# A fixed order on three engines for the first feed-forward product, with each weight block loaded fewer times

## The chip, the cores and the metric

The kernel runs on one core of a Trainium2 chip. The metric is the time of one execution on the device in microseconds, as the median of several runs. PE is TensorE, DVE is VectorE, ACT is ScalarE, POOL is GpSimd and SP is SyncE; PEld is the row of TensorE's weight loads.

## The reference

The reference is one layer of a streaming encoder with 512 tokens and a width of 2048. An S5 branch and a differential attention branch are gated and added to `x`; after them comes a SwiGLU feed-forward with a hidden width of 5632, which is where the change lies. All is float32.

```python
h = rms_norm(x, norm2_w[l], RMS_EPS)
x = x + (jax.nn.silu(h @ w_ffn_gate[l]) * (h @ w_ffn_up[l])) @ w_ffn_down[l]
```

## The kernel before

Each float32 product is computed in three passes: both operands are split into a high part (`hi`, which ACT rounds with a copy) and a rest (`lo`, which DVE gets by subtracting `hi`), and TensorE computes hi*hi, hi*lo and lo*hi. The method `split` does this for a weight chunk of two 128-row blocks by 512 columns: one instruction on ACT (`whi`) and one on DVE (`wlo`).

The first product of the feed-forward, `h @ [gate, up]`, is done in 11 units (`NU = DFF // T`, unit `u` covers 512 hidden columns of `gate` and of `up`). Within a unit the product is a 2 by 2 block scheme with seven block products instead of eight (Winograd's form of Strassen's scheme). The weights' blocks are `w11` and `w21` (the two halves of the rows of `gate`) and `w12` and `w22` (those of `up`). The products 1 to 7 use `w11`, `w21`, `w22`, and sums of blocks: 7 uses `w12 + w22`, 5 uses `w11 + w12`, 6 adds `w22` to that, 4 adds `w21` to that. The slab `A` holds the running sum. Each block product has four chunks of 12 matmuls: two token halves by two 128-row blocks by three passes. Products 6, 3 and 4 accumulate on the PSUM banks of 1, 5 and 7.

The method `seven` (L1044) issues the chunks of a unit in the order it is given, `(1, (2, 7), 5, (6, 3), 4)` for units 1 to 10; products in one bracket alternate chunk by chunk. For each chunk it calls `weights`, which issues the loads (on SP's queue) and the sums (on DVE), and then the split. Product 4's `w21` is added to `A` in flight by a DMA on POOL's queue (L1317). After a product's last chunk `done` copies or adds its banks to the partial results in the tiles `st` and `act` (L1330 to L1353). After every chunk that is not of product 1, one entry of a list `fill` is issued: four flips of the unit before (`flip_act`: four transposes into a bank and a copy by ACT), five empty entries, and the seven steps of `make`. A step of `make` forms one of the seven operands of the second product out of the flipped unit, splits it into two tiles of the pool `wk` (five tiles, two of which hold the gate for part of the unit) and stores both in DRAM (`opd`, L1271, on POOL's queue), from where the second product (`down`) reads it.

TensorE's instructions stand in the order written. Those of the other engines and queues are ordered by a planner at compile time, which goes by priorities and a model of the times; `behind` ties some steps of `make` behind the latest split. Split weights lie in three pairs of tiles, so a chunk's split waits until the chunk three before it has left TensorE. Loaded blocks lie in a ring of five tiles (`raw`: three of the pool `wp`, two parts of `E`). Unit 0 has its own order, `(1, 7, 2, 5, (6, 3), 4)`, and the operands' preparation beside it; the second product follows unit 10 with the same `seven`.

Of the kernel before, what the change touches and what calls it, by code (L numbers as in the profile page):

```python
# [8 lines left out]
F32 = mybir.dt.float32  # L9
F32R = mybir.dt.float32r  # L10
# [7 lines left out]
P = 128  # L18
# [23 lines left out]
class Block:  # L42
# [998 lines left out]

    OWN = {1: ("lin", "lin"), 7: ("lin", "lin"), 2: ("S", "S"), 5: ("S", "S")}

    def seven(self, n, weights, ops, done, order=ORDER, fill=(), own=OWN):  # L1044

        nc = self.nc
        banks = {}  # L1050
        fill = list(fill)
        for group in order:
            group = group if isinstance(group, tuple) else (group,)
            for i in group:
                banks[i] = [self.bank(t) for t in own[i]] if i in own else banks[{6: 1, 3: 5, 4: 7}[i]]
            for c in range(0, n, 2):
                for i in group:
                    raw = weights(i, c)

                    self.nc3 = (self.nc3 + 1) % 3 if self.fp else 1  # L1060
                    hi, lo = (self.wp.tile([P, 2, T], F32R, tag=t, name=self.uid(t)) if self.nc3 else
                              self.fp.tile([P, 2, T], F32R, tag=t, name=self.uid(t)) for t in ("whi", "wlo"))
                    self.last = self.split(hi, lo, raw)
                    for tt, kk in ((tt, kk) for tt in range(2) for kk in range(2)):
                        k = c + kk
                        xh, xl = (ops[i][:, h, k, tt * P:(tt + 1) * P] for h in range(2))
                        for q, (l, r) in enumerate(((xh, hi), (xh, lo), (xl, hi))):
                            nc.tensor.matmul(banks[i][tt], l, r[:, kk, :], skip_group_check=True,  # L1068
                                             start=(i in own and k == 0 and q == 0), stop=(k == n - 1 and q == 2))
# [148 lines left out]
    def flips(self, parts):  # L1218
# [4 lines left out]
            self.nc.tensor.transpose(tp[:, h * P:(h + 1) * P], z, self.ident)  # L1223
        return tp

    def ffn(self, ops, steps, x2d, out):
        nc, a, tc = self.nc, self.a, self.tc
        NU = DFF // T
# [23 lines left out]
        def flip_act(u, j):  # L1252

            tp = self.flips([act[u, tt][:, j * P:(j + 1) * P] for tt in range(4)])
            nc.scalar.activation(self.E[:, 4 + j], tp, AF.Copy)

        flips_act = lambda u: [lambda j=j: flip_act(u, j) for j in range(4)]

        def make(u):

            x1, x2 = self.E[:, 4:6], self.E[:, 6:8]
            a, b = slice(0, 256), slice(256, 512)

            def step(i, x, op=None):
                def f():
                    if op:
                        self.behind(op())
                    hl = [self.work((P, 2, 256), F32R) for _ in range(2)]
                    self.behind(self.split(*hl, x))
                    for h in range(2):  # L1270
                        pool.dma_start(opd[u, i - 1, :, h], hl[h].bitcast(F32))  # L1271
                return f
# [10 lines left out]
        for u in range(NU):  # L1283
            w = {(k + 1, m + 1): (gate, up)[m][k * 1024:(k + 1) * 1024, u * T:(u + 1) * T] for k in range(2) for m in range(2)}
            st = {}
            first = u == 0

            def weights(i, c):
                for _ in range(2 if i == 2 else 1):
                    if steps:  # L1290
                        steps.pop(0)()
                b = lambda k, m: w[k, m][c * P:(c + 2) * P, :]
                if i == (5 if first else 1) and c == 0:
                    if self.A is None:
                        self.A = self.slab("s5", (P, 8, T), F32)
                A = None if self.A is None else self.A[:, c:c + 2]
                if i == 1:
                    return load(raw() if first else A, b(1, 1))
                if i == 2:
                    return load(raw(), b(2, 1))  # L1300
                if i == 3:
                    return st["w22"]
                if i == 7:
                    r1, r2 = load(raw(), b(1, 2)), load(raw(), b(2, 2))
                    add(dve, r2, r1, r2)
                    if not first:
                        add(dve, A, A, r1)
                    return r2
                if i == 5:
                    if first:  # L1310
                        load(A, b(1, 1))
                        add(dve, A, A, load(raw(), b(1, 2)))
                elif i == 6:
                    st["w22"] = load(raw(), b(2, 2))
                    add(dve, A, A, st["w22"])
                else:
                    pool.dma_start(A, two(b(2, 1)), accum_op=ALU.add)  # L1317
                return A

            def done(i, banks):  # L1320
                if first and i == 6:
                    self.E, self.ring = self.slab("s1", (P, 8, T), F32), 2
                if i == 2 and first or i == 6 and u == NU - 1:
                    self.ring = 0
                for tt in range(2):
                    r = lambda th: self.r2[:, 2 * th + tt:2 * th + tt + 1]
                    p = banks[tt]
                    if i == 1:
                        st["x", tt] = self.work()
                        nc.scalar.activation(st["x", tt], p, AF.Copy)  # L1330
                    elif i == 2:
                        g = st["g", tt] = st["x", tt]
                        add(dve, g, g, p)
                        nc.scalar.activation(g, g, AF.Silu, scale=r(0))
                    elif i == 7:
                        st["q"] = banks
                    elif i == 5:
                        d = st["d", tt] = self.fw() if tt else self.spare("row")
                        nc.scalar.activation(d, p, AF.Copy)
                        add(dve, d, d, st["q"][tt], ALU.subtract)  # L1340
                    elif i == 6:
                        x = st["x", tt] = self.spare(("c16", "s16")[tt])
                        nc.scalar.activation(x, p, AF.Copy)
                        add(dve, st["d", tt], st["d", tt], x, ALU.subtract)
                    elif i == 3:
                        o = act[u, tt] = self.fw()
                        add(dve, o, p, st["x", tt], ALU.subtract)
                        dve.scalar_tensor_tensor(o, o, r(0), st["g", tt], op0=ALU.mult, op1=ALU.mult)
                    elif i == 4:
                        x, d = st["x", tt], st["d", tt]  # L1350
                        add(dve, x, x, p)
                        nc.scalar.activation(x, x, AF.Silu, scale=r(1))
                        dve.scalar_tensor_tensor(d, d, r(1), x, op0=ALU.mult, op1=ALU.mult)  # L1353
                        act[u, 2 + tt] = d
# [147 lines left out]
```

## Time and profile before

| | us |
|---|---|
| median of 3 runs | 2575.45 (2575.34 to 2577.14) |
| the profiled execution | 2580.43 |
| its span, first to last instruction | 2578.7 |
| unit 0 of the first product, about | 1250 to 1334 of the span |
| units 1 to 10 | 1334 to 2129 |
| the second product of the feed-forward | 2129 to 2578.7 |

The span is that of one profiled execution. A busy share counts the time in which an engine has an instruction in work; matmuls overlap in the records. A wait is the idle time of an engine before an instruction, put down to what released it. A tile's name stands for its tag: `whi` and `wlo` are split weights, `wk` a work tile, `lin`, `S`, `T` and `O` are PSUM banks, `s` stands for several slabs (among them `A` and `E`), and `raw` for loaded blocks.

### The profile page before, as it was taken

What the parts mean: (1) busy time and instruction counts of PE and PEld (TensorE: products, weight loads), DVE (VectorE), ACT (ScalarE), POOL (GpSimd) and SP (SyncE); (2) the same over time, 40 slices, a digit from 0 to 9 for tenths busy, and PEclk for the clock granted to TensorE, in tenths of its full rate; (3) what the DMA queues carried; (4) which work ended last, traced back from release to release, by engine and by line L of the source; (5) the groups of instructions that cost most, each with busy time, mean ns of one, the idle gap of its engine ahead of it and who ended that gap; (6) DMA issues with size and microseconds to landing.
All of it is one profiled execution on the core that took longest, in us unless ns stands there. A gap on an engine that the chain in (4) does not pass through costs nothing.

```text
span 2578.7 us, 32198 instructions
## 1 busy us (share of the span) xinstructions
PE 2515.2 (98%) x11655; PEld 2050.2 (80%) x11655; DVE 1907.5 (74%) x3024; ACT 1149.1 (45%) x1540; POOL 316.2 (12%) x491
## 2 busy tenths in 40 slices
PE   8999999999999999999999999999999999999999
PEld 7788887877787678888777888878887887788787
DVE  7888854577777775535778787787777778788788
ACT  4123343354455543323545555555554556333332
POOL 1022310000111110000001111111101111000000
PEclk9999999999999999999999999999999999999999
DMA  6545564666753434433767667767667687867775
GB/s 191 158 131 147 142 200 152 222 219 204 253 192 103 130 119 147 159 115 131 240 166 215 199 197 211 209 196 221 190 205 209 197 288 257 254 205 230 245 230 150
DMA packets 258447, 491.84 MB, mean 191 GB/s; under 512 B 43448, under 2 KB 47864, under 8 KB 258288
## 3 DMA queue, kind: packets, MB, share of 16 engines
q1 hardware_dynamic: 196208, 352.50, 42.2%
q0 software_dynamic: 49504, 133.04, 18.7%
q10 hardware_dynamic: 12576, 4.24, 0.8%
q8 instruction: 92, 1.51, 0.2%
q14 instruction: 67, 0.55, 0.1%
HBM read 420.35 MB, written 71.96 MB: 191 GB/s over the span
## 4 chain that ended last, share of the span: by engine, by line
issue 54%; PE 27%; POOL 7%; DVE 5%; DMA 5%; ACT 1%; ACTq 0%; POOLq 0%; DVEq 0%
PE lin L522 21%; POOL opd L1271 3%; DMA raw<-in_w_in_dram 3%; DVE wlo L531 2%; POOL s L1317 2%; PE lin L1068 1%; POOL s L1426 1%; DVE raw L1082 1%; PE S L715 1%; PE O L745 1%; PE S L472 1%; ACT whi L530 1%; PE S L414 1%; PE S L476 0%; DMA s<-in_w_ffn_down_dram 0%
## 5 line engine op out<-in xcount | busy, mean ns | idle before, releaser
L1068 PE MATMUL lin<-whi,s 128*128 128x512 f32 x2400 | 769.9, 391 | 2.0 <-ACT whi L530 2.0
L522 PE MATMUL lin<-s,whi 128*128 128x512 f32 x2432 | 747.1, 397 | 16.5 <-ACT s L536 7.2
L530 ACT ACTIVATE whi<-s 128x1024 fp32r<-128x1024 f32 x351 | 370.1, 1059 | 424.2 <-PE lin L1068 168.4
L522 PEld LDWEIGHTS lin<-s,whi 128*128 128x128 f32 x2432 | 454.9, 190 | 126.8 <-issue 14.9
L531 DVE TENSOR_TENSOR wlo<-s,whi 128x1024 fp32r<-128x1024 f32 x351 | 428.0, 1222 | 137.6 <-ACT whi L530 136.6
L1068 PEld LDWEIGHTS lin<-whi,s 128*128 128x128 f32 x2400 | 450.7, 188 | 95.9 <-ACT whi L530 3.3
L1068 PE MATMUL lin<-wlo,s 128*128 128x512 f32 x1200 | 470.2, 392 | 10.5 <-DVE wlo L531 10.4
L522 PE MATMUL lin<-s,wlo 128*128 128x512 f32 x1216 | 455.4, 393 | 0.0
L500 DVE TENSOR_TENSOR wlo<-raw,whi 128x1024 fp32r<-128x1024 f32 (+1 forms) x153 | 186.0, 1217 | 211.5 <-ACT whi L499 204.6
L499 ACT ACTIVATE whi<-raw 128x1024 fp32r<-128x1024 f32 (+1 forms) x153 | 161.0, 1053 | 356.7 <-PE lin L522 327.5
L1068 PE MATMUL S<-whi,s 128*128 128x512 f32 x976 | 319.4, 393 | 0.2 <-ACT whi L530 0.2
L530 ACT ACTIVATE whi<-raw 128x1024 fp32r<-128x1024 f32 x190 | 200.0, 1058 | 231.0 <-PE lin L1068 75.6
L1068 PEld LDWEIGHTS lin<-wlo,s 128*128 128x128 f32 x1200 | 225.4, 188 | 65.2 <-DVE wlo L531 19.5
L531 DVE TENSOR_TENSOR wlo<-raw,whi 128x1024 fp32r<-128x1024 f32 x190 | 230.2, 1222 | 58.9 <-ACT whi L530 58.4
L522 PEld LDWEIGHTS lin<-s,wlo 128*128 128x128 f32 x1216 | 230.1, 189 | 48.5
L1068 PEld LDWEIGHTS S<-whi,s 128*128 128x128 f32 x976 | 184.0, 189 | 38.1 <-ACT whi L530 0.6
L1068 PE MATMUL S<-wlo,s 128*128 128x512 f32 x488 | 191.7, 393 | 7.9 <-DVE wlo L531 7.8
L1271 POOL DMA_DIRECT2D opd<-wk x154 | 91.2, 618 | 733.7 <-ACT wk L530 634.6
L1068 PE MATMUL T<-whi,s 128*128 128x512 f32 x400 | 139.7, 390 | 0.5 <-ACT whi L530 0.5
L1068 PE MATMUL O<-whi,s 128*128 128x512 f32 x400 | 139.5, 389 | 0.0
L1068 PEld LDWEIGHTS S<-wlo,s 128*128 128x128 f32 x488 | 92.1, 189 | 29.7 <-DVE wlo L531 11.6
L1233 DVE TENSOR_TENSOR s<-s,raw 128x1024 f32<-128x1024 f32 x79 | 96.5, 1222 | 12.5 <-DMA raw<-in_w_ffn_up_dram 11.3
(409 smaller groups left out, 2741.4 us busy)
## 6 DMA issues: line engine op xcount, KB each, us to landing
raw<-in_w_in_dram SPq DMA_DIRECT2D x175, 512.0 KB, 4.3
raw<-in_w_ffn_up_dram SPq DMA_DIRECT2D x83, 512.0 KB, 4.5
opd<-wk POOLq DMA_DIRECT2D x154, 256.0 KB, 4.5
s<-opd SPq DMA_DIRECT2D x77, 512.0 KB, 9.1
s<-in_w_ffn_down_dram SPq DMA_DIRECT2D x65, 512.0 KB, 6.3
s<-in_w_ffn_gate_dram SPq DMA_DIRECT2D x60, 512.0 KB, 5.0
s<-in_w_ffn_up_dram SPq DMA_DIRECT2D x48, 512.0 KB, 4.2
s<-in_w_ffn_gate_dram POOLq DMA_DIRECT2D x44, 512.0 KB, 8.1
```

Source lines behind the costliest of these rows:

```text
L414: nc.tensor.matmul(mb[:, q * 32:(q + 1) * 32], w1[:, ri, q].rearrange("p k c -> p (k c)"), self.cd[:, ri, q].rearrange("p g c -> p (g c)") ...
L472: state = lambda ri, **kw: nc.tensor.matmul(y[:, q * P:(q + 1) * P], w2[:, ri, q].rearrange("p k c -> p (k c)"), sd[:, ri, q].rearrange("p ...
L499: nc.scalar.activation(hi[:, ks], raw[:, ks], AF.Copy)
L500: nc.vector.tensor_tensor(lo[:, ks], raw[:, ks], hi[:, ks].bitcast(F32), op=ALU.subtract)
L522: nc.tensor.matmul(acc[b], l, r, start=(k == 0 and i == 0), stop=(k == nk - 1 and i == 2))
L530: ins = self.nc.scalar.activation(hi, x, AF.Copy)
L531: self.nc.vector.tensor_tensor(lo, x, hi.bitcast(F32), op=ALU.subtract)
L715: nc.tensor.matmul(sp[m], qT[ms, h, i * P:(i + 1) * P], kT[ms, h, 0:W], start=True, stop=True)
L1068: nc.tensor.matmul(banks[i][tt], l, r[:, kk, :], skip_group_check=True, start=(i in own and k == 0 and q == 0), stop=(k == n - 1 and q == 2))
L1233: add = lambda eng, o, x, y, op=ALU.add: eng.tensor_tensor(o, x, y, op=op)
L1271: pool.dma_start(opd[u, i - 1, :, h], hl[h].bitcast(F32))
L1317: pool.dma_start(A, two(b(2, 1)), accum_op=ALU.add)
```

## The change

Units 1 to 10 leave `seven` and the loop with `weights` and `done`, and are issued by a new method `units`, inside a block in which DVE and ACT, too, keep the order written. SP's and POOL's queues are still ordered by the planner.

- The products stand in the order `(1, 2), (7, 5, 3, 6), 4`. Product 3 has banks of its own (T and O), product 5 takes the S banks, and an add (`53`) joins them.
- Time is counted in chunks. In step `s` of the loop TensorE gets chunk `s`, ACT and DVE split chunk `s + 2`, and DVE forms the sums for chunk `s + 4`. Between ACT's and DVE's half of the split stand the steps due (`post`): evacuations of banks one to four steps after a product's last chunk (`STAGES`), and pieces of `make`.
- The blocks `w21`, `w12` and `w22` of a unit come once each into the ring of five, a load being issued when its place is given free; `w11` goes into `A` when product 4 has split the chunk of it. Product 4's `w21` still comes by the adding DMA.
- The flips stand after the chunks 4 to 7 of the next unit, with ACT's copy one step later. The steps of `make` start at step 9 of the unit and stand three steps apart; DVE's half and the stores come one step after ACT's half.
- Unit 0 keeps `seven`, with product 3 on banks of its own, so it also does the add `53`.

```diff
-                    hi, lo = (self.wp.tile(...) if self.nc3 else self.fp.tile(...) for t in ("whi", "wlo"))
+                    hi, lo = self.halves()
...
+    def units(self, ops, block, load, stage, stages, flip_act, make):
...
+        order = ((1, 2), (7, 5, 3, 6), (4,))
+        S = [(u, i, c) for u in range(1, NU) for g in order for c in range(0, 8, 2) for i in g]
+        own = {1: ("lin", "lin"), 7: ("lin", "lin"), 2: ("S", "S"), 5: ("S", "S"), 3: ("T", "O")}
...
+        def sums(u, i, c):
+            a = A[:, c:c + 2]
+            if i == 7:
+                add(a, a, w[u, 1, 2, c])
+                add(w[u, 1, 2, c], w[u, 1, 2, c], w[u, 2, 2, c])
+            elif i == 6:
+                add(a, a, w[u, 2, 2, c])
+
+        def taken(u, i, c):
+            if i == 2:
+                give(u, 2, 1, c)
+            elif i == 7:
+                give(u, 1, 2, c)
+            elif i == 3:
+                give(u, 2, 2, c)
+            elif i == 6:
+                nc.gpsimd.dma_start(A[:, c:c + 2], block(u, 2, 1, c).rearrange("(k p) c -> p k c", p=P), accum_op=ALU.add)
+            elif i == 4 and u + 1 < NU:
+                base(u + 1, c)
...
+            for f, s in zip(make(u - 1, lambda f: at(self.slot + 1, f)), range(s0 + 9, s0 + 40, 3)):
+                at(s, f)
...
+        for s in range(-4, len(S) + 4):
+            self.slot = s
+            if 0 <= s + 2 < len(S):
+                x = src(*S[s + 2])
+                hl[s + 2] = self.halves()
+                nc.scalar.activation(hl[s + 2][0], x, AF.Copy)
+            for f in post.pop(s, ()):
+                f()
+            if 0 <= s + 2 < len(S):
+                hi, lo = hl[s + 2]
+                self.last = nc.vector.tensor_tensor(lo, x, hi.bitcast(F32), op=ALU.subtract)
+                taken(*S[s + 2])
...
+            if 0 <= s + 4 < len(S):
+                sums(*S[s + 4])
+            loads()
+            if 0 <= s < len(S):
...
+                self.chunk(banks[i], ops[i], *hl.pop(s), c, 8, i in own)
...
+        STAGES = {1: ((1, "1"),), 2: ((1, "2"), (2, "gate1")), 7: (), 5: ((1, "5"), (2, "57")), 3: ((2, "53"),),
+                  6: ((1, "6"), (2, "o"), (3, "d"), (4, "act1")), 4: ((1, "4"), (2, "gate2"), (3, "act2"))}
...
-            order = (1, 7, 2, 5, (6, 3), 4) if first else (1, (2, 7), 5, (6, 3), 4)
-            self.seven(8, weights, ops, done, order, flips_act(u - 1) + [lambda: None] * 5 + make(u - 1) if u else (),
-                       own={**self.OWN, 5: ("T", "O")})
+        self.seven(8, weights, ops, done, (1, 7, 2, 5, (6, 3), 4), own={**self.OWN, 5: ("T", "O"), 3: ("S", "S")})
+        with tc.manual_schedule(engines={mybir.EngineType.PE, mybir.EngineType.DVE, mybir.EngineType.Activation}):
+            self.units(ops, block, load, stage, STAGES, flip_act, make)
```

More of the change, by code (lines that the diff above doesn't have):

```diff
@@ L1042, with halves, chunk @@
     OWN = {1: ("lin", "lin"), 7: ("lin", "lin"), 2: ("S", "S"), 5: ("S", "S")}
+    def halves(self):
+        self.nc3 = (self.nc3 + 1) % 3 if self.fp else 1
+        return [(self.wp if self.nc3 else self.fp).tile([P, 2, T], F32R, tag=t, name=self.uid(t)) for t in ("whi", "wlo")]
+    def chunk(self, banks, op, hi, lo, c, n, own):
+        for tt, kk in ((tt, kk) for tt in range(2) for kk in range(2)):
+            k = c + kk
+            xh, xl = (op[:, h, k, tt * P:(tt + 1) * P] for h in range(2))
+            for q, (l, r) in enumerate(((xh, hi), (xh, lo), (xl, hi))):
+                self.nc.tensor.matmul(banks[tt], l, r[:, kk, :], skip_group_check=True,
+                                      start=(own and k == 0 and q == 0), stop=(k == n - 1 and q == 2))
     def seven(self, n, weights, ops, done, order=ORDER, fill=(), own=OWN):
@@ L1058, in seven @@
                     raw = weights(i, c)
-                    self.nc3 = (self.nc3 + 1) % 3 if self.fp else 1
-                    hi, lo = (self.wp.tile([P, 2, T], F32R, tag=t, name=self.uid(t)) if self.nc3 else
-                              self.fp.tile([P, 2, T], F32R, tag=t, name=self.uid(t)) for t in ("whi", "wlo"))
+                    hi, lo = self.halves()
                     self.last = self.split(hi, lo, raw)
[L1064 to L1069, printed above, removed]
+                    self.chunk(banks[i], ops[i], hi, lo, c, n, i in own)
                     if c == n - 2:
@@ L1250, in load, with flip_act, make @@
             return dst
[L1252 removed]
+        def flip_act(u, j, later=lambda f: f()):
             tp = self.flips([act[u, tt][:, j * P:(j + 1) * P] for tt in range(4)])
[L1255 removed]
+            later(lambda: nc.scalar.activation(self.E[:, 4 + j], tp, AF.Copy))
         flips_act = lambda u: [lambda j=j: flip_act(u, j) for j in range(4)]
[L1259 removed]
+        def make(u, later=None):
             x1, x2 = self.E[:, 4:6], self.E[:, 6:8]
@@ L1264, in step, with store, low, f @@
             def step(i, x, op=None):
[L1265 to L1269, printed above, removed]
+                def store(hl):
                     for h in range(2):
                         pool.dma_start(opd[u, i - 1, :, h], hl[h].bitcast(F32))
+                def low(hl):
+                    add(dve, hl[1], x, hl[0].bitcast(F32), ALU.subtract)
+                    store(hl)
+                def f():
+                    o = op() if op else None
+                    hl = [self.work((P, 2, 256), F32R) for _ in range(2)]
+                    if later:
+                        nc.scalar.activation(hl[0], x, AF.Copy)
+                        later(lambda: low(hl))
+                    else:
+                        if o:
+                            self.behind(o)
+                        self.behind(self.split(*hl, x))
+                        store(hl)
                 return f
@@ L1281, in make @@
                     step(4, x22)]
[L1283 to L1315, printed above, removed]
-                else:
[L1317 to L1354, printed above, removed]
-            order = (1, 7, 2, 5, (6, 3), 4) if first else (1, (2, 7), 5, (6, 3), 4)
-            self.seven(8, weights, ops, done, order, flips_act(u - 1) + [lambda: None] * 5 + make(u - 1) if u else (),
-                       own={**self.OWN, 5: ("T", "O")})
@@ new lines, in ffn, with weights @@
+        block = lambda u, k, m, c: (gate, up)[m - 1][(8 * k - 8 + c) * P:(8 * k - 6 + c) * P, u * T:(u + 1) * T]
+        st = {}
+        def weights(i, c):
+            for _ in range(2 if i == 2 else 1):
+                if steps:
+                    steps.pop(0)()
+            b = lambda k, m: block(0, k, m, c)
+            if i == 5 and c == 0:
+                self.A = self.slab("s5", (P, 8, T), F32)
+            A = None if self.A is None else self.A[:, c:c + 2]
+            if i == 1:
+                return load(raw(), b(1, 1))
+            if i == 2:
+                return load(raw(), b(2, 1))
+            if i == 3:
+                return st["w22"]
+            if i == 7:
+                r1, r2 = load(raw(), b(1, 2)), load(raw(), b(2, 2))
+                add(dve, r2, r1, r2)
+                return r2
+            if i == 5:
+                load(A, b(1, 1))
+                add(dve, A, A, load(raw(), b(1, 2)))
+            elif i == 6:
+                st["w22"] = load(raw(), b(2, 2))
+                add(dve, A, A, st["w22"])
+            else:
+                pool.dma_start(A, two(b(2, 1)), accum_op=ALU.add)
+            return A
@@ new lines, in ffn, with done @@
+        STAGES = {1: ((1, "1"),), 2: ((1, "2"), (2, "gate1")), 7: (), 5: ((1, "5"), (2, "57")), 3: ((2, "53"),),
+                  6: ((1, "6"), (2, "o"), (3, "d"), (4, "act1")), 4: ((1, "4"), (2, "gate2"), (3, "act2"))}
+        def done(i, banks):
+            if i == 6:
+                self.E, self.ring = self.slab("s1", (P, 8, T), F32), 2
+            if i == 2:
+                self.ring = 0
+            for tt in range(2):
+                st[f"p{i}", tt] = banks[tt]
+            if i != 3:
+                for _, name in STAGES[i]:
+                    if name not in ("o", "act1"):
+                        stage(0, st, name)
+            else:
+                for name in ("53", "o", "act1"):
+                    stage(0, st, name)
```

76 lines of the change are left out of this document (added).

## The prediction

> **What bounds the kernel now.** I read the engines' totals first, then the stretch that the change rewrites (units 1 to 10 of the first feed-forward product) by windows, then single matmuls, then the waits, and last one stall from the transfer that starts it to TensorE. First the page's totals, then busy time in windows of that stretch (length, then busy us and instructions of PE, PEld, DVE, ACT, POOL, the granted clock, DMA share, GB/s). Each window runs from the first matmul of a unit's product 2 to that of the next unit's; the last ends with the stretch; "sum" adds eleven windows, the first of them the four chunks of unit 1's product 1.
>
> ```profile
> PE 2515.2 (98%) x11655; PEld 2050.2 (80%) x11655; DVE 1907.5 (74%) x3024; ACT 1149.1 (45%) x1540; POOL 316.2 (12%) x491
> ...
> 1345.00:1426.07 81.07, 79.12 (x353) 64.42 (x352) 63.21 (x66) 41.09 (x49) 12.74 (x18) 1.00 0.70 207
> 1426.07:1505.05 78.98, 78.53 (x353) 64.50 (x352) 62.22 (x65) 41.09 (x49) 12.65 (x18) 1.00 0.71 208
> ...
> 1662.98:1743.43 80.45, 78.88 (x353) 64.41 (x352) 62.40 (x65) 41.07 (x49) 12.66 (x18) 1.00 0.69 203
> ...
> 2061.46:2129.30 67.84, 67.56 (x305) 55.56 (x304) 52.88 (x56) 34.91 (x42) 12.75 (x18) 1.00 0.88 280
> sum 795.18, PE 786.93 PEld 644.87 DVE 621.38 ACT 411.06 POOL 126.93; mean PE 71.54 PEld 58.62 DVE 56.49 ACT 37.37 POOL 11.54
> ```
>
> TensorE bounds the kernel, and its clock is full (1.00). The question is how much of these 795.2 us is lost. Matmul records overlap, so I take it from their pace: two starts 24 matmuls apart where nothing waits, and two starts around a chunk that has a flip (four transposes) behind it.
>
> ```profile
> 1305.04 0.39 PE L1068 MATMUL lin<-whi,s 128*128 128x512 f32 x1
> ...
> 1310.48 0.39 PE L1068 MATMUL lin<-whi,s 128*128 128x512 f32 x1
> ...
> 1348.08 0.48 PE L1068 MATMUL lin<-whi,s 128*128 128x512 f32 x1
> ...
> 1351.30 0.48 PE L1068 MATMUL S<-whi,s 128*128 128x512 f32 x1
> ```
>
> The first pair of rows is two chunks apart, so a chunk of 12 matmuls takes 5.44/2 = 2.72 us; I call that a slot. The second pair shows 3.22 us with a flip, so a flip costs 0.50. A unit is 7 products of 4 chunks and 4 flips: 28 x 2.72 + 4 x 0.50 = 78.16 us at least. Ten units need 781.6 and took 795.2: 13.6 us are lost. The windows show it unit by unit: 2.9 in unit 1, 0.8 in unit 2, 2.3 in the one from 1662.98. By busy time the loss would look like 795.18 - 786.93 = 8.3 us.
>
> The Trainium skill, page "Perfetto Trace Analysis", section "Identifying the Most-Contended Engine", calls matmul busy time a poor measure of headroom since matmuls are pipelined; the two numbers above agree (8.3 by busy time, 13.6 by pace), and by busy time the sum below would end 5.3 us higher.
>
> Now the waits inside 1334 to 2129 us (waiter, what it waited for, total us, times, longest): first what held up TensorE's weight loads, then what held up the two engines that feed it.
>
> ```profile
> PEld lin L1068 <- DVE wlo L531: 8.3, 12, 1.4
> PEld T L1068 <- DVE wlo L531: 7.6, 9, 1.1
> PEld T L1068 <- ACT whi L530: 0.9, 1, 0.9
> ...
> ACT wk L530 <- DMA opd<-wk: 57.6, 21, 4.4
> ...
> DVE wk L531 <- DMA opd<-wk: 21.0, 15, 4.4
> DVE raw L1233 <- DMA raw<-in_w_ffn_up_dram: 19.2, 12, 3.2
> DVE s L1233 <- DMA s<-in_w_ffn_up_dram: 13.7, 15, 1.5
> DVE s L1233 <- DMA raw<-in_w_ffn_up_dram: 8.2, 12, 2.0
> ```
>
> TensorE waits only for split weights, 22 times, never for a bank or a transfer of its own. ACT and DVE wait for stores of `opd` to land (78.6 us) and DVE for weights (41.1 us). One stall, followed through the timelines of ACT, DVE, PE and PEld:
>
> ```profile
> 1709.37 0.63 ACT L530 ACTIVATE wk<-s 128x512 fp32r<-128x512 f32 x1 [2.45 <-DMA opd<-wk]
> ...
> 1710.98 1.23 DVE L531 TENSOR_TENSOR wlo<-raw,whi 128x1024 fp32r<-128x1024 f32 x1 [2.41 <-ACT whi L530]
> ...
> 1712.26 0.19 PEld L1068 LDWEIGHTS T<-wlo,s 128*128 128x128 f32 x1 [1.01 <-DVE wlo L531]
> ...
> 1714.40 0.69 DVE L531 TENSOR_TENSOR wk<-s,wk 128x512 fp32r<-128x512 f32 x1 [1.06 <-DMA opd<-wk]
> ...
> 1714.90 0.39 PE L1068 MATMUL lin<-whi,s 128*128 128x512 f32 x1
> ...
> 1716.28 0.19 PEld L1068 LDWEIGHTS lin<-wlo,s 128*128 128x128 f32 x1 [1.41 <-DVE wlo L531]
> ...
> 1715.10 1.06 ACT L530 ACTIVATE whi<-s 128x1024 fp32r<-128x1024 f32 x1 [2.26 <-PE O L1068]
> ```
>
> ACT stands at a piece of `make` (the split of the unit's output) because the work tile it writes is still being stored to `opd`; the weight split behind it comes late, so does DVE's half, and the array idles about 1 us. `make` issues its seven steps in seven slots in a row, with five work tiles of which two hold the gate.
>
> **The change, part by part.** Durations used (busy us, then mean ns of one; after the bar idle time before them):
>
> ```profile
> L531 DVE TENSOR_TENSOR wlo<-s,whi 128x1024 fp32r<-128x1024 f32 x208 | 253.3, 1222 | 73.5 <-ACT whi L530 73.0
> ...
> L531 DVE TENSOR_TENSOR wk<-s,wk 128x512 fp32r<-128x512 f32 x70 | 48.2, 689 | 22.0 <-DMA opd<-wk 21.0 <-ACT whi L530 1.0
> ...
> L1348 DVE SCALAR_TENSOR_TENSOR fw<-fw,rs,wk 128x512 f32<-128x512 f32 x20 | 15.0, 748 | 0.0
> ...
> L530 ACT ACTIVATE whi<-s 128x1024 fp32r<-128x1024 f32 x208 | 219.4, 1058 | 197.7 <-PE lin L1068 67.9 <-PE O L1068 50.1 <-PE S L1068 34.5
> ...
> L530 ACT ACTIVATE wk<-s 128x512 fp32r<-128x512 f32 x70 | 43.8, 626 | 74.5 <-DMA opd<-wk 57.6 <-DVE s L1233 12.9 <-DVE wlo L531 3.7
> ```
>
> TensorE: 28 chunks and 4 flips a unit as before; nothing gained or lost in its own work. Product 3 gets banks of its own, so 2 adds of 0.69 a unit are new on DVE; they are read off the path below. Loads: 20 transfers of 512 KB a unit in place of 24 (w22 no longer comes twice, w12 still once, and four of the twenty still add in flight through POOL). The DMA share of 0.7 leaves room either way, so the fewer bytes I cost at nothing.
>
> The order on DVE. A slot gives DVE 2.72 us. In slot s ACT splits chunk s+2 once chunk s-1 has left TensorE (three buffer pairs): 0.2 after the slot's start in the row at 1715.10 against the matmul at 1714.90, plus 1.06, so DVE's half can start at about 1.5 at the latest. It must be done when chunk s+2 asks for it, 5.44 + 0.23 later than the slot's start. The heaviest place is slots 7 to 9 of a unit. Slot 7: split to 2.7, one sum (1.22) to 3.9, that is 1.2 into slot 8. Slot 8: two adds of product 2's banks to 2.6, split to 3.8, two sums to 6.2, that is 3.5 into slot 9. Slot 9: split to 4.7, against 5.67. It holds by 1.0 us. Slots 24 to 28 carry about 3.3 each (two adds, a piece of `make`, a split), and no sums, so the split there ends at 4.4 or earlier. In all DVE gets 68 instructions for the 66 of a unit before, some 64 us of 78: no stall from its own work. Banks: product 5 starts in slot 9 on those that the two adds of slot 8 empty, the first at 1.9, due at 2.72; product 4 starts in slot 24 on those read in slot 23.
>
> `make` goes to every third slot, 8.2 us apart, its DVE half one slot later. The first tile of a step is wanted again by the next step's DVE half, so a store has about 8.1 us. The sum transfer for product 4 gets tighter: chunk 6 of A is free when product 6's last split ends (2.7 into slot 21) and product 4 needs it split by slot 27: 6 x 2.72 - 2.7 - 2.2 (both halves) = 11.4 us, one slot less than before. The next unit's first block has 4 x 2.72 - 2.3 = 8.6 us to ACT's split, and that split has a further slack of 2. Times from issue to landing, min/median/max: stores of `opd` (these units), sum transfers on POOL (these units), all loads of SP (whole feed-forward):
>
> ```profile
> DMA to landing us min/median/max: 2.3/4.2/9.6
> ...
> DMA to landing us min/median/max: 5.9/8.4/9.5
> ...
> DMA to landing us min/median/max: 3.5/4.8/13.7
> ```
>
> Medians clear all three, and the sum transfers clear even at their longest. POOL's queue is passed by the same 14 stores and 4 sums a unit, 12.7 us of 78. On SP a load waits for a buffer that DVE's split frees; nothing more urgent stands behind it, since the sums for a chunk are due five slots (13.6 us) later. If the stalls from `make` go, the sum transfer is late next, with 1.9 us to spare.
>
> Unit 0 keeps the planner, but gets the two adds too: 0 to 1.4 us; I take 1.4, since TensorE waits for DVE there (rows below). The entry into the fixed order: between 0 and unit 1's loss before, 2.9; I take 1.0, as the mean unit lost 1.4. The third product's order is planned anew by unchanged code: it could gain or lose; its waits, and unit 0's above them:
>
> ```profile
> PEld T L1068 <- DVE wlo L531: 3.1, 3, 2.0
> PEld lin L1068 <- DVE wlo L531: 2.9, 3, 1.5
> ...
> PEld lin L1068 <- DVE wlo L531: 7.4, 9, 1.7
> PEld S L1068 <- DVE wlo L531: 5.9, 5, 1.3
> PEld lin L1068 <- ACT whi L530: 3.3, 4, 2.4
> ```
>
> I take 0 there, between -2.5 and +2.5, the spread that equal units show among themselves (78.9 to 81.1, rounded up).
>
> The sum: -13.6 + 1.4 + 1.0 = -11.2 us. The profiled execution took 2580.43 us (span 2578.7), 5.0 above the median of 2575.45; it would be 2569.2, and the median 2564.3.
>
> **Rivals.** (a) Half the loss stays. DVE waited 41.1 us for weights beside 78.6 for stores; if the spacing cures stores only, 41.1/119.7 = 34% of 13.6 us, 4.7, remain: 2569. For it: the loads still go through a ring of five. Against: each now has five slots.
> (b) The gain is lost further on. If the third product's waits (16.6 in its three rows) grow by half, 8.3 us return: 2564.3 + 8.3 = 2572.6, within 0.2% of before. For it: the planner's order there depends on what is ready. Against: its code and its input times hardly change.
> (c) Slower: a transfer that comes late at the head of a queue whose order is now fixed. The place is the sum transfer for product 4's last chunk, the point 11.4 us. Were it as slow as SP's slowest load, 13.7, each unit would lose 2.3 us, ten 23: 2587. Against: 40 of them took 5.9 to 9.5.
> The Trainium skill, page "TensorE: Matmul & The Clock Gate", section "Architectural detail: the array is 16× 32×32, not 1× 128×128", states that ScalarE's and VectorE's queues are strictly first in, first out; the rows at 1709 to 1716 agree, and it is why (c) has a chance of its own.
>
> **How the numbers follow.** A measurement here tells about 0.2%, 5.2 us, from no change. The sum's case 0.60, whose own range is 2559 (all 13.6 back and 2.5 in the third product) to 2569; (a) 0.13; (b) 0.16; (c) 0.11. Faster by over 0.2% (below 2570.3) is the sum's case and most of (a), 0.70; same 0.18; slower 0.12. The range 2559 to 2577 leaves out most of (c) and a little below.
>
> **What would show it.** Unit windows of 78.2 to 78.8 us; TensorE's waits for split weights in the units under 4 us in place of 16.8; ACT's and DVE's waits for `opd` near 0; no wait of ACT for the POOL sums. It is wrong if units still take 79 us or more, if the first matmuls of product 5 wait for S banks, if splits in slot 9 come late, or if the time past 2129 us grows.

## The result, and the profile after

| | before | after |
|---|---|---|
| median of 6 runs, us | 2578.94 (2575.34 to 2581.35) | 2564.69 (2560.87 to 2570.00) |
| ratio, 95% interval | 1 | 0.9949 (0.9933 to 0.9964) |
| profiled execution, us (span) | 2580.43 (2578.7) | 2570.00 (2568.2) |
| unit 0, first matmul to unit 1 | 70.7 | 69.9 |
| units 1 to 10 | 795.2 | 780.8 |
| second product, to the end | 449.4 | 453.3 |

The kernel is 0.51% faster (0.36 to 0.67%), 13 us by the ratio; the two profiled executions are 10.5 us of span apart. A repeat beside later runs gave 0.9954 (0.9941 to 0.9967).

First the page's totals after, then windows of the changed kernel (length, then busy us and instructions of PE, PEld, DVE, ACT, POOL, the granted clock, DMA share, GB/s): units 1 to 10, two short stretches at the start of the second product, and the second product as a whole.

```profile
PE 2513.2 (98%) x11655; PEld 2055.4 (80%) x11655; DVE 1927.1 (75%) x3046; ACT 1145.1 (45%) x1540; POOL 316.5 (12%) x491
...
1334.08:2114.87 780.79, 780.79 (x3522) 646.33 (x3521) 640.60 (x670) 407.08 (x490) 127.19 (x180) 1.00 0.66 186
...
2120.50:2124.00 3.50, 1.22 (x6) 0.61 (x5) 3.50 (x5) 0.98 (x2) 0.00 (x0) 0.99 0.02 5
2124.00:2127.50 3.50, 3.50 (x10) 2.74 (x9) 2.28 (x3) 1.65 (x2) 0.00 (x0) 0.52 0.45 150
2114.87:2568.20 453.33, 437.24 (x1929) 356.10 (x1927) 374.04 (x412) 177.42 (x185) 31.60 (x34) 0.99 0.70 223
```

In units 1 to 10 PE is busy for the whole 780.79 us, where it was for 786.93 of 795.18 before, and a unit takes 78.08. The page's totals do not show it: 98% then and now. Of the waits in these units, these are the rows of DVE and ACT that matter; no row of PE or PEld is left, and nothing waits for a store to `opd`.

```profile
DVE wlo L1306 <- ACT whi L1301: 135.0, 147, 2.3
...
ACT whi L1301 <- DMA raw<-in_w_ffn_up_dram: 4.9, 3, 1.7
...
ACT whi L1301 <- DMA s<-in_w_ffn_gate_dram: 0.9, 1, 0.9
```

The 3.9 us given back lie behind unit 10. From the first flip in the second product to the second flip (2120.31 to 2127.86) the changed kernel takes 7.6 us, where the kernel before takes 3.2 (2134.75 to 2137.93). The timelines there, of PE and then of DVE:

```profile
2121.92 0.33 PE L1229 MATMUL O<-ident,fw 128*128 128x128 f32 x1 [1.12 <-DVE fw L1464]
2122.02 0.47 PE L1055 MATMUL lin<-whi,s 128*128 128x512 f32 x1
2123.65 0.57 PE L1055 MATMUL lin<-wlo,s 128*128 128x512 f32 x1 [1.16 <-DVE wlo L531]
2124.01 1.05 PE L1055 MATMUL lin<-whi,s 128*128 128x512 f32 x2
...
2119.98 1.22 DVE L531 TENSOR_TENSOR wlo<-s,whi 128x1024 fp32r<-128x1024 f32 x1
2121.12 0.74 DVE L1464 SCALAR_TENSOR_TENSOR fw<-fw,rs,s 128x512 f32<-128x512 f32 x1
2121.78 0.68 DVE L1334 TENSOR_TENSOR s<-s,S 128x512 f32<-128x512 f32 x1
2122.38 1.22 DVE L531 TENSOR_TENSOR wlo<-raw,whi 128x1024 fp32r<-128x1024 f32 x1
```

The first flip of unit 10 waits for the last gating (`fw`, L1464), the first chunk of product 7 for its split (`wlo<-raw`); on DVE a split of a later product stands ahead of both. DVE has work without a gap from 2109.9 to 2124.7; before, it stood idle for 1.7 us ahead of the split at 2123.9, 5.4 us before the second product began. Then TensorE runs at half its clock: 0.52 granted in the second short window, matmuls 427 ns apart.

### The profile page after: what moved, and what is told of

Same layout as the page of the kernel before. It is cut to its first block, busy times and chain, and to the rows that moved or that the text cites. A ratio compares the mean times of both kernels' runs of the same rounds, so it can differ in the third digit from the quotient of the medians.

```text
span 2568.2 us, 32111 instructions
## 1 busy us (share of the span) xinstructions
PE 2513.2 (98%) x11655; PEld 2055.4 (80%) x11655; DVE 1927.1 (75%) x3046; ACT 1145.1 (45%) x1540; POOL 316.5 (12%) x491
## 4 chain that ended last, share of the span: by engine, by line
PE 43%; issue 39%; POOL 6%; DVE 5%; DMA 5%; ACT 1%; POOLq 0%; ACTq 0%; SPq 0%; DVEq 0%
PE lin L522 30%; PE lin L1055 5%; POOL opd L1369 3%; DMA raw<-in_w_in_dram 3%; PE S L1055 2%; DVE wlo L531 2%; POOL s L1280 1%; POOL s L1556 1%; PE S L715 1%; ACT whi L530 1%; DVE raw L1088 1%; PE S L472 1%; PE O L745 1%; PE S L414 1%; PE S L476 0%
## 5 line engine op out<-in xcount | busy, mean ns | idle before, releaser
L522 PEld LDWEIGHTS lin<-s,whi 128*128 128x128 f32 x2432 | 455.3, 190 | 127.7 <-issue 14.8
L1055 PEld LDWEIGHTS lin<-whi,s 128*128 128x128 f32 x2400 | 452.3, 188 | 96.0 <-ACT whi L530 2.8
L1055 PE MATMUL S<-whi,s 128*128 128x512 f32 x1328 | 436.0, 393 | 0.2 <-ACT whi L530 0.2
L1055 PEld LDWEIGHTS S<-whi,s 128*128 128x128 f32 x1328 | 250.5, 189 | 52.3 <-ACT whi L530 0.6
L1055 PE MATMUL S<-wlo,s 128*128 128x512 f32 x664 | 260.5, 392 | 8.5 <-DVE wlo L531 8.5
L531 DVE TENSOR_TENSOR wlo<-raw,whi 128x1024 fp32r<-128x1024 f32 x118 | 142.1, 1220 | 32.6 <-ACT whi L530 32.1
L1055 PEld LDWEIGHTS S<-wlo,s 128*128 128x128 f32 x664 | 125.4, 189 | 37.0 <-DVE wlo L531 11.8
```

The costliest lines, as they stand in the source:

```text
L522: nc.tensor.matmul(acc[b], l, r, start=(k == 0 and i == 0), stop=(k == nk - 1 and i == 2))
L531: self.nc.vector.tensor_tensor(lo, x, hi.bitcast(F32), op=ALU.subtract)
L1055: self.nc.tensor.matmul(banks[tt], l, r[:, kk, :], skip_group_check=True, start=(own and k == 0 and q == 0), stop=(k == n - 1 and q == 2))
```

## The experiments

Each was run beside the kernel before on its chip. "Nine units" is the time from the first flip in unit 1 to that in unit 10; a window of that length gives it for the two kernels, before and after:

```profile
sum 716.46, PE 708.49 PEld 580.29 DVE 560.38 ACT 369.98 POOL 114.17; mean PE 708.49 PEld 580.29 DVE 560.38 ACT 369.98 POOL 114.17
...
sum 702.68, PE 702.68 PEld 581.69 DVE 577.14 ACT 366.28 POOL 114.50; mean PE 702.68 PEld 581.69 DVE 577.14 ACT 366.28 POOL 114.50
```

The first number is the length. So 13.8 us are to be explained. Theory: the stalls came from `make` standing at stores of `opd`, and its new spacing cured them. Rivals: it is the order on DVE and ACT, or the fewer loads.

**Spaced make alone, in the old loop.**

```diff
-flips_act(u - 1) + [lambda: None] * 5 + make(u - 1) if u else ()
+flips_act(u - 1) + [lambda: None] + [g for f in make(u - 1) for g in (f, lambda: None, lambda: None)][:-2] if u else ()
```

> The kernel before with one edit: the seven steps of make stand at every third entry of the fill list (5, 8, ... 23) in place of seven in a row; loads, product order and the planner's order on DVE and ACT stay. Units 1 to 10 took 795.2 us before and 780.8 after the change. Spacing theory (ACT and DVE wait for stores to opd, 78.6 us): ACT's and DVE's waits for opd fall below 10 us and most of the 14.4 us come back, units 782 to 785, the kernel 10 to 13 us below before. Rival (a), the loads count too: a third of the loss stays, units 786 to 788, 8 to 9 us below. Fixed-order theory (it is the order on DVE and ACT that saves the time): units 791 or more, within 4 us of before.

Ratio to before 0.9996 (0.9983 to 1.001): nothing. Its nine units, one bad unit, its waits, and that unit's stall in the timelines of DVE, SP and PEld:

```profile
1345.78:2062.79 717.01, 707.27 (x3170) 582.08 (x3168) 562.19 (x586) 369.05 (x441) 114.08 (x162) 1.00 0.70 205
1742.52:1825.47 82.95, 80.25 (x354) 65.63 (x352) 62.86 (x66) 41.12 (x49) 12.66 (x18) 0.98 0.70 203
...
DVE raw L1233 <- DMA raw<-in_w_ffn_up_dram: 38.5, 19, 5.7
...
DVE s L1233 <- DMA s<-in_w_ffn_up_dram: 28.5, 18, 4.5
PEld T L1068 <- DVE wlo L531: 13.5, 9, 3.1
...
1788.87 1.22 DVE L1233 TENSOR_TENSOR raw<-raw,raw 128x1024 f32<-128x1024 f32 x1 [5.66 <-DMA raw<-in_w_ffn_up_dram]
1790.01 1.22 DVE L531 TENSOR_TENSOR wlo<-s,whi 128x1024 fp32r<-128x1024 f32 x1
...
1779.91 0.37 SPq L1249 DMA_DIRECT2D raw<-in_w_ffn_up_dram  x1
...
1791.28 0.19 PEld L1068 LDWEIGHTS T<-wlo,s 128*128 128x128 f32 x1 [3.12 <-DVE wlo L531]
```

The waits for `opd` are gone, as the theory said, and the time did not move. In the units 1 to 9 one stall each is left, always at the third chunk of product 3, and it has another origin: the planner put the sum for the next unit's product 7 on DVE ahead of this chunk's split, and that sum's load, issued at 1779.91, landed at 1788.9. DVE waits for weights 76 us (38.5 + 28.5 + 9.3) where it had waited 41. A wait took the place of the one removed, at about the same size. (Behind the longest stall TensorE ran at half clock for 3.4 us, the 0.98 in the second row; that is at most 1.7 us of the 717.)

**Spaced make with the sums tied behind the splits.** As above, and in units 1 to 10 each sum stands behind the split of the chunk before.

```diff
-add(dve, A, A, st["w22"])
+o = add(dve, A, A, st["w22"])
+if not first:
+    self.behind(o)
```

> The run with spaced make alone, with one more edit: in units 1 to 10 each sum of weight blocks is tied behind the split of the chunk before it, so that the planner can't put it earlier on DVE; the planner orders the rest. In the run with spaced make alone no engine waited for opd any more, and the loss sat in one stall a unit (0.85 to 3.1 us, nine times): DVE stood at the sum for the next unit's product 7, whose load was still landing, with product 3's split behind it. Theory Q (two causes, stores at the head of ACT's queue and early sums at the head of DVE's): the stall goes, units 1 to 10 at 782 to 785 us, the kernel 9 to 13 us below before. Rival (only a whole fixed order does it): units stay at 790 or more, within 4 us of before.

Ratio 0.9967 (0.9954 to 0.9979). Nine units, and the waits that are left:

```profile
sum 709.16, PE 704.35 PEld 581.30 DVE 562.57 ACT 367.24 POOL 113.46; mean PE 704.35 PEld 581.30 DVE 562.57 ACT 367.24 POOL 113.46
...
PEld S L1068 <- DVE wlo L531: 7.1, 6, 2.4
...
DVE s L1233 <- DMA s<-in_w_ffn_up_dram: 25.2, 12, 3.4
DVE raw L1233 <- DMA raw<-in_w_ffn_up_dram: 25.1, 18, 3.2
```

The stall at product 3 is gone and 7.3 of the 13.8 us are back. Neither theory's number is met (units at 782 to 785, or 790 and more; the nine at 709 make about 787 for ten). So one cause is shown: sums at the head of DVE's queue, 7.9 us against the run before (717.01 to 709.16). That stores at the head of ACT's queue are the other one in the old loop is read from the waits only; a run with the sums tied and `make` still in a row was not made. All waits left are at splits of product 2; at the longest, 2.4 us, a sum whose load was still landing stood ahead of the split on DVE (3.4 us idle at 1599).

**The changed kernel with DVE and ACT given back to the planner.**

```diff
-with tc.manual_schedule(engines={mybir.EngineType.PE, mybir.EngineType.DVE, mybir.EngineType.Activation}):
+with tc.manual_schedule(engines={mybir.EngineType.PE}):
```

> The changed kernel with one edit: only TensorE keeps the order written, DVE and ACT are ordered by the planner again; product order, single loads and spaced make stay. Spacing theory: units 1 to 10 stay at 781 to 784 us, the kernel within 3 us of the changed one. Fixed-order theory: the stalls come back, units 790 or more, the kernel 8 to 14 us above the changed one. Of the third product's start both say nothing; the planner may order it otherwise, -4 to +2 us.

Ratio to before 1.0086 (1.0073 to 1.01): slower than before by 22 us. Nine units, and what TensorE's weight loads waited for:

```profile
sum 731.92, PE 713.73 PEld 582.41 DVE 572.60 ACT 371.04 POOL 114.40; mean PE 713.73 PEld 582.41 DVE 572.60 ACT 371.04 POOL 114.40
...
PEld S L1055 <- DVE wk L1334: 15.2, 10, 2.4
PEld lin L1055 <- DVE wlo L1306: 9.8, 10, 1.4
PEld lin L1055 <- ACT whi L1301: 4.7, 7, 1.5
```

The new product order needs the S banks emptied within one slot, and the planner does not do that: product 5 waits for them once in every unit. Without the order on DVE and ACT the nine units take 29 us more, and the kernel is over 30 us above the changed one, more than the 8 to 14 expected. ACT and DVE waited for stores of `opd` again, too (53.4 and 7.9 us): the planner did not keep the spacing (the steps of `make` start 2.4 to 7.2 us apart on ACT), so the run takes away both.

**The changed kernel with make in a row.**

```diff
-range(s0 + 9, s0 + 40, 3)
+range(s0 + 13, s0 + 20)
```

> The changed kernel with one edit: the seven steps of make stand in seven steps in a row (13 to 19 of a unit) in place of every third; the fixed order, product order and single loads stay. Spacing theory: a step's tile is still being stored when the next step writes it (store landing 4.2 us against a slot of 2.72), and in a fixed order the splits stand behind it: each of seven steps is late by about 2 us, less some 3 us of slack, 2 to 12 us a unit, the kernel 20 to 120 us above the changed one, with ACT's or DVE's waits for opd the largest. Fixed-order theory: units stay at 781 to 784.

Ratio 1.0461 (1.0448 to 1.0475), 119 us above before. Its rows:

```profile
sum 817.02, PE 742.81 PEld 598.92 DVE 580.27 ACT 366.55 POOL 113.91; mean PE 742.81 PEld 598.92 DVE 580.27 ACT 366.55 POOL 113.91
...
DVE wk L1334 <- DMA opd<-wk: 106.6, 32, 8.2
...
PEld S L1055 <- DVE wlo L1306: 53.2, 18, 5.1
```

12.7 us a unit are lost, a little more than was expected. Part of it is the clock: 0.96 was granted over these units, which is at most some 33 of the 114 us (an estimate, 4% of 817). In the planner's order the same seven steps in a row cost at most the 1.4 us a unit of the kernel before. A fixed order does not remove a late operand; it makes everything behind it pay. The spacing alone brought nothing in the old loop, and the order without the spacing does harm; in the changed kernel both are needed.

**Steps of make two apart.** `range(s0 + 9, s0 + 40, 2)`.

> The changed kernel with the steps of make two steps apart (5.4 us) in place of three (8.2). Spacing theory: a store lands 4.2 us after its issue (2.3 to 9.1), so most steps find their tile free; ACT's and DVE's waits for opd appear but stay under 15 us in all, units 1 to 10 at 781 to 784 us. The last unit ends with less left on DVE, so the second product's start may lose 0 to 2 us less than its 4. A threshold theory (the spacing must exceed a store's longest landing, 9.1): units 785 or more.

Ratio 0.9956 (0.9941 to 0.997). Nine units took 702.68 us, as with three apart, although waits for stores appear:

```profile
ACT wk L1379 <- DMA opd<-wk: 9.0, 9, 3.2
...
DVE wk L1334 <- DMA opd<-wk: 3.0, 4, 1.2
```

5.4 us of spacing against a median landing of 4.2 suffices; 12 us of waits are hidden by the two chunks of lead. The second product did not gain: the first flip waited 3.6 us there instead of 1.4.

**As many loads as before.** Four copies of 512 KB a unit from a block of `w22` to an unread place in DRAM, on SP's queue.

```diff
+if 0 <= s < len(S) and S[s][1] == 6:
+    nc.sync.dma_start(idle[s // 4 % 4], block(S[s][0], 2, 2, S[s][2]).rearrange("(k p) c -> p k c", p=P))
```

> The changed kernel with 4 more transfers of 512 KB a unit on SP's queue (a block of w22 copied to a place in DRAM that nobody reads), so that a unit issues 24 as before. If the fewer loads matter by their number or bytes, units 1 to 10 go from 780.8 to 785 us or more; by the sum of the prediction, which costs them at nothing, they stay at 780.8 to 782 and the kernel within 2 us of the changed one.

Inconclusive: nine units took 702.67 us, the kernel 0.9972 (0.9962 to 0.9983) of before, but the copies did not run in the units. SP's queue is the planner's, and it issued all 40 at the start of the kernel (duration in ns, then first and last start in us):

```profile
L1315 SPq DMA_DIRECT2D idle<-in_w_ffn_up_dram x40: 542/548/2256, 19.2 to 127.0; - x40
```

So whether the fewer loads are needed beside the order and the spacing is left open. Alone they are not enough: in the run with DVE and ACT given back to the planner, which has the fewer loads, DVE waited 84.5 us for weights (36.6 + 26.7 + 14.8 + 6.4), more than the 41 before. The new product order was never taken away by itself.

**Two more instructions on DVE in step 8 of each unit**, repeats of the split's second half, ahead of the sums.

```diff
+if s % 28 == 8:
+    for _ in range(2):
+        nc.vector.tensor_tensor(lo, x, hi.bitcast(F32), op=ALU.subtract)
```

> The changed kernel with two repeats of the DVE half of a split (1.22 us each) in step 8 of each unit, ten units. The prediction's ledger has 1.0 us to spare in slot 9 by durations; back to back DVE starts them 1.14 apart, which leaves about 1.5. By durations each unit is late by 1.3 us (13 in all), by pace by 0.7 (7 in all); if the order has more slack than the ledger says, nothing. If DVE's load were no limit at all, no stall at any place.

```profile
sum 705.96, PE 705.49 PEld 581.41 DVE 596.82 ACT 366.08 POOL 114.51; mean PE 705.49 PEld 581.41 DVE 596.82 ACT 366.08 POOL 114.51
...
PEld lin L1055 <- DVE wlo L1306: 5.0, 10, 0.7
```

Each unit is late once, by 0.36 us (705.96 - 702.68 over nine). 2 x 1.14 us were added, so the slack there was 1.9 us, not 1.0: the ledger found the right place and was 0.9 too strict.

**The adding transfer three steps later.**

```diff
-nc.gpsimd.dma_start(A[:, c:c + 2], ...)
+at(self.slot + 3, lambda: nc.gpsimd.dma_start(A[:, c:c + 2], ...))
```

> The changed kernel with product 4's adding transfer issued three steps later than the place becomes free; for the last chunk of each unit that cuts its time from 11.4 us to 11.4 - 3 x 2.72 = 3.3 us, while such a transfer lands in 6.1 us (5.8 to 8.8). If the ledger's budget is right, ACT waits for it and each unit is late by 2.8 us, or by 1.9 if this ledger too is 0.9 too strict, as it was for DVE (two repeats cost 0.36 us a unit in place of 1.3): 19 to 28 us in all. If the fixed order had slack that the ledger doesn't know, less than 10.

Inconclusive: nine units 702.68 us, ratio 0.9957 (0.9942 to 0.9973), but the edit moved nothing. The transfers' first and last start, after and in this run:

```profile
L1280 POOL DMA_DIRECT2D s<-in_w_ffn_gate_dram x40: 1177/1235/1276, 1364.1 to 2098.7; - x40
...
L1280 POOL DMA_DIRECT2D s<-in_w_ffn_gate_dram x40: 1177/1235/1276, 1361.9 to 2096.5; - x40
```

Counted from the first flip of unit 1 (1347.68 and 1345.46) both start at 16.4 us. POOL's queue is still the planner's, and it issues the transfer when its place is free, wherever the line stands. What a late sum transfer would cost is left open.

**The start of the second product, three tries.** With ACT's splits tied to the order of the chunks there:

```diff
+new = self.split(hi, lo, raw)
+if self.tied and i != order[0]:
+    self.behind(new)
```

> The changed kernel with one edit: in the second feed-forward product ACT's splits are tied to the order of the chunks (the planner had put the split of product 5's first chunk before that of product 7's). Theory P, the planner's reversal makes the wait at 2122 us: the wait for wlo there (1.16) goes, the one of the flip (1.12) gets shorter, and the stretch at half clock behind them (1.8 us lost) goes with them: the second product 450 to 451 us in place of 453.3, the kernel 2 to 3.5 us below the changed one. Rival D, DVE itself is full there (busy without a gap from 2109.9 to 2124.7): within 1 us of the changed one.

Ratio 0.9965 (0.9954 to 0.9977). Start to start, the first flip's gap fell from 1.39 to 0.35 us, that of product 7's split rose from 1.63 to 2.23; from the first flip to the second it took 7.1 us in place of 7.6, and the second product 456.1. The reversal by the planner is not the cause.

With the flips one chunk later and make's steps two apart (`fill = [lambda: None] + flips_act(NU - 1)`):

> The changed kernel with make's steps two apart and unit 10's flips one chunk later in the second product (behind product 7's chunk in place of product 2's). With the steps two apart alone the flip waited 3.6 us at 2114.5 for the last gating on DVE, while the split for product 7 was ready 0.6 us after TensorE asked for it; behind product 7 the flip finds the gating nearly done. If the wait of the flips is what the second product lost (453.3 us in place of 449.4), 3 us come back: 445 to 446 us from the first flip's old place to the end, where the run with steps two apart had 448.4. If DVE's load is the bound there, the wait moves to the split of the next chunk and less than 1 us comes back.

Ratio 0.995 (0.9937 to 0.9962). The second product, and the waits of weight loads in its first 28 us and in the 65 us after them:

```profile
2106.93:2562.60 455.67, 438.01 (x1929) 355.73 (x1927) 373.85 (x412) 177.21 (x185) 31.75 (x34) 0.99 0.70 222
...
PEld lin L1055 <- DVE wlo L531: 1.3, 3, 0.5
...
PEld lin L1055 <- DVE wlo L531: 4.7, 4, 1.7
PEld lin L1055 <- ACT whi L530: 3.8, 3, 2.3
```

The waits at the start fell to 1.3 us (2.9 in the changed kernel), and the product as a whole took 455.7 us in place of 453.3: most of it was lost again at the change to the next pass, some 80 us on, where TensorE fell to half clock (as it did there in the changed kernel, at 2202). The third try adds the tie to it:

> The run with late flips and, in the second product's first pass, ACT's splits tied to the order of the chunks, so that product 7's split stays ahead of product 5's whatever the planner finds. If the planner keeps that order by itself in the run with late flips, the same time within 1 us; if not, 1 to 3 us less.

Ratio 0.9958 (0.9946 to 0.9971), the second product 454.7 us. None of the three beats the changed kernel, which was run beside the last two:

> The changed kernel itself, on the chip of the runs beside it: 0.994 to 0.996 of before. Units 1 to 10 at 780.8 us again, the second product's start with the same waits.

Ratio 0.9954 (0.9941 to 0.9967); units 1 to 10 at 780.79 us again, the second product at 454.9. No version here is faster than the changed kernel by more than the intervals.

Other runs tell more of the loss at the start of the second product. With DVE and ACT given back to the planner the first flip there is 3.2 us ahead of the second, as before, and the second product takes 450.8 us: the loss comes with the fixed order. In the run with the copies, whose second product has the code of the changed kernel, the same two waits stand at 2117.90 and 2119.63, and no half clock follows. Its windows over the waits and behind them:

```profile
2116.70:2120.20 3.50, 1.41 (x8) 0.77 (x6) 3.50 (x5) 0.95 (x2) 0.00 (x0) 1.00 0.02 5
2120.20:2123.70 3.50, 3.50 (x19) 2.89 (x18) 2.28 (x3) 2.78 (x4) 0.00 (x0) 1.00 0.51 150
```

There the two flips are 5.8 us apart. So of the 4.4 us that the changed kernel lost at this place, the waits are 2.6 and the half clock most of the rest, and the half clock comes in some executions and not in others.

## Why the prediction was right or wrong, point by point

- **The loss in the units**, 13.6 us from the pace of the matmuls: right, 14.4 came back. The minimum of 78.16 us a unit was 0.08 too high (a flip costs 0.48, not 0.50). By busy time, 8.3 us, it would have been missed by 6.
- **What makes the loss**: half right. The stores of `opd` stood at the head of ACT's queue, but curing them alone brings nothing, since sums on DVE that wait for loads then cost the same. Rival (a), that a third of the loss would stay if only the stores were cured (its heading says half), used the right mechanism and a wrong size: in the old loop all of it stays. In the changed kernel none does. There the sums stand behind the split and four chunks ahead of their use, which is the likely reason; the fewer loads may have a part in it, and no run tells.
- **The ledger of slots**: right in its verdict and its place; the slack in slot 9 is 1.9 us and not 1.0. (DVE gets 67 instructions a unit for 65 by the counts over ten units, not 68 for 66.)
- **Spacing of make, stores 8.1 us against 4.2**: right; two steps apart would do as well.
- **Fewer loads at nothing**: untested, since the copies that were to show it ran elsewhere.
- **Unit 0, +1.4, and the entry, +1.0**: wrong, both are nothing. Unit 0 took 0.8 us less than before and unit 1 its 78.1 from the first chunk.
- **The second product, 0 with ±2.5**: this term was mis-sized; it lost 3.9, outside its bounds. The bound was taken from the spread of equal units, but the term is not one of them: the fixed order leaves DVE more to do at the end of unit 10 than the planner did, and waits can bring TensorE's clock down behind them. Over the profiled executions with fixed order, spaced `make` and this second product it took 452.3 to 455.0 us, and behind the old loop 447.6 to 449.4. Rival (b) had named the stretch; half of its price came. And a sign of being wrong that the prediction had set, a longer time past the units, did come.
- **The sum**: -11.2 us forecast, -10.5 between the profiled executions and -13 by the runs. By terms it is -14.4 in the units, -0.8 in unit 0, +3.9 in the second product, and +0.8 ahead of unit 0, which the change leaves as it was. It is right in part by luck: the 3.9 lost and the 2.4 that were not lost in unit 0 and the entry, with 0.8 more from the units, largely cancel. That the median of 2564.69 meets the forecast of 2564.3 is luck as well, since the kernel before took 2578.94 in the median of six runs, 3.5 more than the forecast started from.
- **Rival (c)**: not seen (ACT waited for the adding transfers once, 0.9 us); the run that was to bring it about left the transfers where they were. But its mechanism, a late operand in a fixed queue, is what the run with make in a row shows, at 12.7 us a unit, with stores in its place.

## What to carry to other kernels

Before an engine's order is fixed, give every transfer that an instruction in it waits for more time than the transfer takes to land in the median, since in a fixed order all that stands behind pays; here two chunks of lead and 5.4 us of spacing made ten units run without one idle slot, and with a spacing of one slot the kernel was 119 us slower than before. When one wait is cured and the time does not move, look for what stands next at the head of the queues that feed the bound engine. Look in the trace whether an edit moved what it was to move, when a planner orders the queue: two edits here did not do so in the units. And count an end of a stretch as a term of its own: the last unit's leftovers met the next stage's first chunks.

## What the runs showed of the hardware

Behind the two waits at the start of the second product matmuls came 427 ns apart in place of 227 for 3.4 us, at half the granted clock; eight or nine matmuls then lose about 1.7 us. In each of the traces here the changes of the granted clock lie on a grid of 3.41 us. The changed kernel by that grid, over the waits, behind them, and at the change to the next pass (the same two windows there):

```profile
2120.52:2123.93 3.41, 1.13 (x6) 0.58 (x5) 3.41 (x5) 0.96 (x2) 0.00 (x0) 1.00 0.02 5
2123.93:2127.35 3.42, 3.42 (x9) 2.65 (x9) 2.20 (x3) 1.65 (x2) 0.00 (x0) 0.50 0.46 153
...
2199.03:2202.44 3.41, 1.70 (x7) 1.00 (x6) 2.24 (x2) 2.00 (x2) 0.00 (x0) 1.00 0.31 120
2202.44:2205.85 3.41, 3.41 (x10) 2.66 (x9) 3.41 (x5) 0.04 (x1) 0.00 (x0) 0.50 0.44 154
```

TensorE was busy for 33% and 50% of the windows ahead of the two drops. In the kernel before, waits of 2.4 and 1.3 us at 2208 to 2212 fell into two windows, 2206.40 to 2209.81 and 2209.81 to 2213.23, busy for 66% and 55%, and the clock stayed full; so it did in the run with the copies, where both waits touch the window 2115.78 to 2119.19, busy for 52%. How the waits fall on the grid differs between executions, which is the likely reason that the same waits bring the half clock in one and not in another. The Trainium skill, page "TensorE: Matmul & The Clock Gate", Part 1, section "What's actually happening", names half clock after an idle window of about 3.4 us and says that the window runs freely. The half clock, its length and the grid agree with the traces, but here windows in which TensorE was busy for a third to a half of the time were idle enough. No limit comes out of the busy shares: the clock also fell behind a window busy for 66% (857.59 to 861.00 of the changed kernel), and stayed full behind one busy for 44% (1749.12 to 1752.53 of the run with `make` in a row).
